# Row means on one core: the loop's loads issued by GpSimd as single packets instead of by SyncE

## The chip, the cores and the metric

The kernel runs on one core of one Trainium2 chip. A core has the engines PE (TensorE, unused here), DVE (VectorE), ACT (ScalarE), POOL (GpSimd) and SP (SyncE), which run their own instruction streams and meet at semaphores, and 16 DMA engines that move data between HBM and the on-chip memory of 128 partitions. The metric is the device time of one execution in microseconds (us). Lower is better.

## The reference

```python
x = np.random.randn(64, 256, 8192).astype(np.float32)

def reference(x):
    return np.mean(x, axis=2)
```

16,384 rows of 8,192 float32 values, 536.87 MB, are read once; 16,384 means are written.

## The kernel before

The 16,384 rows are spread over 128 partitions, 128 rows to each partition. A partition's rows lie in two zones, of 111 and 17 rows, and rows that follow each other in a zone are contiguous in HBM. Two buffers take the rows: `four` holds four rows for each partition (128 KB, 16.78 MB over all), `two` holds two (64 KB, 8.39 MB). There is no second copy of either, so that a load into one runs while the other is being reduced.

SP issues every load, on one hardware queue, in this order:

- three pieces into `two` (a row at the border of the zones and one ahead of it, L109 to L111), then the first `four` load (L112, semaphore `second_sem`);
- the loop of 17 rounds (L114): wait until `two` is free, load two rows into it (L116, `two_sem`), wait until `four` is free, load four rows into it (L118, `four_sem`). Both waits take their count back with a decrement;
- the rest, unrolled (`REST`, L121 to L131): two and four rows in turn, waits with constants; then the last two rows in five chunks that grow shorter (L136), and the two stores.

DVE reduces both rows of `two` with one tensor_reduce (`pair`, L169), then three rows of `four` by adding the halves of a row and accumulating the sum (`quad`, `halves`, L151). In the loop it waits for `two_sem` (L183), reduces, waits for `go_sem` (L185), which ACT raises when `four` has landed, and for `turn_sem` (L186), writes its three sums into `turn`, and copies them to the results (L189). Ahead of the loop DVE reduces the first `two` and then waits for the first `four` load (L179). ACT sums the fourth row of `four` by an activation with an accumulated output (L218), in the loop after a wait on `four_sem` (L224). `two_free` counts finished `pair`s; `four_free` gets one count from DVE and one from ACT for each `four` that is done, and SP waits for both.

GpSimd does little: it sets `turn_sem`, clears one column (L89), and scales the results to means, first the 111 of the large zone (L91, after `four_free` has reached 4 in the rest), then the others (L97).

All of the loop's waits on a load compare with 16, since each load adds 16 to its semaphore, one for each DMA engine, and the waiting engine takes the 16 off again.

Of the kernel before, what the change touches and what calls it, by code (L numbers as in the profile page):

```python
# [11 lines left out]
def bass_global_avg_pool_1d_kernel(  # L12
# [6 lines left out]
    B, C, L = x.shape  # L19
# [8 lines left out]
    FROM = [0, ZONE[0]]  # L28
    EARLY, LATE = ZONE
    ROUNDS = (ZONE[0] - 9) // 6  # L30
    REST = [(112, 2), (106, 4), (114, 2), (116, 4), (120, 2)]
    HALF, LASTP = 122, 124
# [12 lines left out]
    zone = [  # L45
        flat[P * f : P * (f + n), :].rearrange("(p r) l -> p (r l)", p=P)
        for f, n in zip(FROM, ZONE)
    ]
# [5 lines left out]
    with ExitStack() as ctx:  # L54
        sb = lambda n, s: ctx.enter_context(nc.sbuf_tensor(n, s, F32))
        sem = lambda n: ctx.enter_context(nc.semaphore(n))
# [7 lines left out]
        four = sb("four", [P, 4 * L])  # L64
        two = sb("two", [P, 2 * L])

        four_sem = sem("four_sem")
        go_sem = sem("go_sem")
        two_sem = sem("two_sem")
        turn_sem = sem("turn_sem")  # L70
        four_free = sem("four_free")
        two_free = sem("two_free")
        first_sem = sem("first_sem")
        second_sem = sem("second_sem")
        chunk_sems = [sem(f"chunk_sem{c}") for c in range(4)]
        owned_sem = sem("owned_sem")
        last_sem = sem("last_sem")
# [6 lines left out]

        eng = nc.gpsimd
        eng.sem_inc(turn_sem, 2)
        eng.memset(part(NPART - 1), 0.0).then_inc(last_sem, 1)  # L89
        eng.wait_ge(four_free, 4)  # L90
        eng.tensor_scalar(  # L91
            scaled[:], res[:, 0:EARLY], inv, None, op0=mybir.AluOpType.mult
# [8 lines left out]


        eng = nc.sync
        def rows_of(n, k):
            z = 1 if n >= FROM[1] else 0
            return zone[z][:, (n - FROM[z]) * L : (n - FROM[z] + k) * L]

        a, z = rows_of(ZONE[0] - 1, 1), rows_of(ZONE[0], 1)
        eng.dma_start(two[:, L : L + FIRST], z[:, 0:FIRST]).then_inc(first_sem, 16)  # L109
        eng.dma_start(two[:, L + FIRST : 2 * L], z[:, FIRST:L]).then_inc(first_sem, 16)  # L110
        eng.dma_start(two[:, 0:L], a).then_inc(first_sem, 16)  # L111
        eng.dma_start(four[:], rows_of(0, 4)).then_inc(second_sem, 16)  # L112
        src = rows_of(4, 6 * ROUNDS).rearrange("p (i w) -> p i w", i=ROUNDS)
        with eng.Fori(0, ROUNDS) as i:  # L114
            eng.wait_ge(two_free, 1).then_inc(two_free, -1)
            eng.dma_start(two[:], src[:, bass.ds(i, 1), 0 : 2 * L]).then_inc(two_sem, 16)  # L116
            eng.wait_ge(four_free, 2).then_inc(four_free, -2)
            eng.dma_start(four[:], src[:, bass.ds(i, 1), 2 * L : 6 * L]).then_inc(  # L118
                four_sem, 16
            )  # L120
        for k, (n, size) in enumerate(REST):  # L121
            if size == 2:
                eng.wait_ge(two_free, k // 2 + 1)
                eng.dma_start(two[:], rows_of(n, 2)).then_inc(two_sem, 16)
            else:
                eng.wait_ge(four_free, 2 * (k // 2 + 1))
                eng.dma_start(four[:], rows_of(n, 4)).then_inc(four_sem, 16)
        eng.wait_ge(four_free, 6)
        eng.dma_start(four[:, 0 : 2 * L], rows_of(HALF, 2)).then_inc(four_sem, 16)
        eng.wait_ge(two_free, 5)  # L130
        eng.dma_start(two[:], rows_of(LASTP, 2)).then_inc(two_sem, 16)  # L131
        last = rows_of(OWN - 2, 2)
        for c in range(5):
            a, z = cuts[c], cuts[c + 1]
# [12 lines left out]
        eng = nc.vector  # L147
# [20 lines left out]
        def pair(to, ap=two[:]):  # L168
            eng.tensor_reduce(to, rows_in(ap), X, ADD).then_inc(two_free, 1)  # L169

        def quad(to, done=four_free):
            for j, ap in enumerate(to):
                halves(
                    four[:, j * L : (j + 1) * L], ap, done if j == len(to) - 1 else None
                )
# [4 lines left out]
        quad([at(j, 1) for j in range(3)])  # L180
        with eng.Fori(0, ROUNDS) as i:
            now = sums[:, bass.ds(i, 1), :]
            eng.wait_ge(two_sem, 16).then_inc(two_sem, -16)  # L183
            pair(now[:, :, 0:2])
            eng.wait_ge(go_sem, 1).then_inc(go_sem, -1)  # L185
            eng.wait_ge(turn_sem, 2).then_inc(turn_sem, -2)  # L186
            quad([turn[:, j : j + 1] for j in range(3)], turn_sem)
            eng.wait_ge(turn_sem, 1).then_inc(four_free, 1)
            eng.tensor_copy(  # L189
                now[:, :, 2:5], turn[:].rearrange("p (i w) -> p i w", i=1)  # L190
            ).then_inc(turn_sem, 1)
        for k, (n, size) in enumerate(REST):
            eng.wait_ge(two_sem if size == 2 else four_sem, 16 * (k // 2 + 1))
            if size == 4:
                quad([at(n, 1), at(n + 1, 1)])
            elif k < len(REST) - 1:
                pair(at(n, 2))
            else:
                pair(at(n, 1), two[:, 0:L])
        eng.wait_ge(four_sem, 48)  # L200
        eng.tensor_reduce(  # L201
            at(HALF, 2), rows_in(four[:, 0 : 2 * L]), X, ADD
        ).then_inc(owned_sem, 1)
        eng.wait_ge(two_sem, 64)
        eng.tensor_reduce(at(LASTP, 1), two[:, 0:L], X, ADD).then_inc(owned_sem, 1)  # L205
        eng.wait_ge(chunk_sems[0], 16)
        halves(tail[:, 0:L], res[:, OWN - 2 : OWN - 1], owned_sem)
# [7 lines left out]
        eng = nc.scalar  # L215

        def row(ap, to):
            return eng.activation(ap, ap, COPY, accum_out=to)  # L218
# [2 lines left out]
        eng.wait_ge(second_sem, 16)  # L221
        row(fourth, at(3, 1)).then_inc(four_free, 1)
        with eng.Fori(0, ROUNDS) as i:
            eng.wait_ge(four_sem, 16).then_inc(four_sem, -16)  # L224
            eng.sem_inc(go_sem, 1)
            row(fourth, sums[:, bass.ds(i, 1), 5:6]).then_inc(four_free, 1)
        for k, (n, size) in enumerate(REST):
            if size == 4:
                eng.wait_ge(four_sem, 16 * (k // 2 + 1))
                row(four[:, 2 * L : 3 * L], at(n + 2, 1))  # L230
                row(fourth, at(n + 3, 1)).then_inc(four_free, 1)
        eng.wait_ge(two_sem, 48)
        row(second, at(REST[-1][0] + 1, 1)).then_inc(two_free, 1)
        eng.wait_ge(two_sem, 64)
        row(second, at(LASTP + 1, 1)).then_inc(owned_sem, 1)
        for c in range(4):
            eng.wait_ge(chunk_sems[c], 16)
# [31 lines left out]
```

## Time and profile before

| | |
|---|---|
| median of 2 runs | 1242.8 us (1242.71 to 1242.89) |
| the profiled execution's own time | 1243.15 us |
| its span, first to last instruction | 1241.8 us |
| DVE, ACT, POOL busy | 52%, 14%, 0% |
| DMA | one hardware queue, 536.94 MB, 99.8% of 16 engines' span |
| mean rate over the span | 432 GB/s |

How to read the lines of the profile: engines are PE, DVE, ACT, POOL and SP; `SPq` and `DVEq` are the sequencers of SP and DVE, where their waits and DMA issues stand. L118 is line 118 of the kernel. In a timeline a line has its start, its duration, engine, line, operation, output and input, the count of instructions, and in brackets the idle time of the engine before it with what ended that. In the waits a line names who waited for whom, and then the total, the number and the longest of the waits. In the groups a line ends with busy time and mean ns of one, then the idle time before. DMA issues have their size and the median time from issue to landing; a landing is the moment at which the load's semaphore is complete. The page cuts the span into 40 slices of 31 us each.

### The profile page before, as it was taken

How to read it: one execution, taken by the hardware profiler on the slowest of the kernel's cores; microseconds unless marked ns; L12 is line 12 of the kernel's file. 1: busy time of each engine (PE TensorE's matmuls, PEld its weight loads, DVE VectorE, ACT ScalarE, POOL GpSimd, SP SyncE). 2: the span in 40 equal slices, each digit the busy share in tenths (PEclk: the TensorE clock that was granted, in tenths of full speed). 3: DMA queues.
4: the chain of work that ended last, by engine and by line, in shares of the span. 5: the costliest groups of instructions: out<-in, count | busy, mean ns of one | idle time of the engine just before them, and what ended most of it. 6: DMA issues, size and time to landing. Idle time of an engine off the chain costs nothing. (4 is left out here: it accounts for less than half of the span.)

```text
span 1241.8 us, 713 instructions
## 1 busy us (share of the span) xinstructions
DVE 643.0 (52%) x166; ACT 176.5 (14%) x57; POOL 2.3 (0%) x7
## 2 busy tenths in 40 slices
DVE  2373836454544637383736454554638383625257
ACT  0021020202020202012020202020202102040423
POOL 0000000000000000000000000000000000000000
DMA  9999999999999999999999999999999999999998
GB/s 405 439 439 439 439 431 414 439 439 439 439 439 422 422 439 439 439 439 439 422 422 439 439 439 439 439 422 422 439 439 439 439 439 424 420 439 439 439 439 374
DMA packets 10048, 536.94 MB, mean 432 GB/s; under 512 B 1088, under 2 KB 1216, under 8 KB 1472
## 3 DMA queue, kind: packets, MB, share of 16 engines
q1 hardware_dynamic: 10048, 536.94, 99.8%
HBM read 536.87 MB, written 0.07 MB: 432 GB/s over the span
## 5 line engine op out<-in xcount | busy, mean ns | idle before, releaser
L151 DVE CUSTOM_DVE_ANT_0 four<-four 128x4096 f32<-128x4096 f32 (+3 forms) x62 | 260.5, 4248 | 434.7 <-DVEq L186 366.7
L169 DVE TENSOR_REDUCE res<-two 128x16384 f32 (+2 forms) x21 | 353.1, 16814 | 145.4 <-DVEq L183 96.3
L218 ACT ACTIVATE four<-four 128x8192 f32<-128x8192 f32 x22 | 154.6, 7029 | 1017.9 <-ACTq L224 864.3
L201 DVE TENSOR_REDUCE res<-four 128x2 f32<-128x16384 f32 x1 | 17.2, 17220 | 10.6 <-DMA four<-in_x_dram 10.6
L218 ACT ACTIVATE two<-two 128x8192 f32<-128x8192 f32 x2 | 14.1, 7030 | 36.7 <-DMA two<-in_x_dram 36.7
L205 DVE TENSOR_REDUCE res<-two 128x1 f32<-128x8192 f32 x1 | 8.7, 8686 | 2.1 <-DMA two<-in_x_dram 2.1
L240 ACT ACTIVATE four<-four 128x2048 f32<-128x2048 f32 (+3 forms) x4 | 4.1, 1030 | 7.7 <-DMA four<-in_x_dram 7.5
L189 DVE COPY res<-turn 128x3 f32 x17 | 2.9, 170 | 4.2 <-DVE turn L151 4.2
L151 DVE DVE_READ_ACCUMULATOR2_ANT turn<- 128x1 f32 x51 | 4.2, 83 | 0.0
L218 ACT ACTIVATION_READ_ACCUMULATOR four<-four (+1 forms) x22 | 4.1, 187 | 0.0
L91 POOL TENSOR_SCALAR scaled<-res 128x111 f32<-128x111 f32 x1 | 0.5, 503 | 1117.6 <-ACT four L218 1117.6
L97 POOL TENSOR_SCALAR ends<-res 128x16 f32<-128x16 f32 x1 | 1.5, 1499 | 117.9 <-DVE res L151 117.9
L218 ACT ACT_TABLE_LOAD x1 | 1.3, 1283 | 0.7 <-PEq L254 0.7
L240 ACT ACTIVATION_READ_ACCUMULATOR four<-four 128x1 f32 x4 | 0.7, 186 | 0.0
L151 DVE DVE_READ_ACCUMULATOR2_ANT res<- 128x1 f32 x8 | 0.7, 82 | 0.0
L151 DVE CUSTOM_DVE_ANT_0 fin<-fin 128x228 f32<-128x228 f32 x1 | 0.4, 397 | 0.2 <-ACT four L240 0.2
L218 ACT ACTIVATION_READ_ACCUMULATOR two<-two 128x1 f32 x2 | 0.4, 186 | 0.0
L151 DVE DVE_READ_ACCUMULATOR2_ANT fin<- 128x1 f32 x3 | 0.2, 82 | 0.0
L254 POOL MEMSET const-bfloat16-1.0<- 128x1 bf16 x1 | 0.1, 101 | 0.0
L254 POOL MEMSET const-uint8-127<- 128x1 uint8 x1 | 0.1, 101 | 0.0
L254 POOL MEMSET const-float32-0.0<- 128x1 f32 x1 | 0.1, 99 | 0.2 <-issue 0.2
L89 POOL MEMSET fin<- 128x1 f32 x1 | 0.1, 98 | 0.4 <-POOLq L254 0.4
(2 smaller groups left out, 0.2 us busy)
## 6 DMA issues: line engine op xcount, KB each, us to landing
four<-in_x_dram SPq DMA_DIRECT2D x1, 5120.0 KB, 41.6
two<-in_x_dram SPq DMA_DIRECT2D x1, 4096.0 KB, 20.9
two<-in_x_dram SPq DMA_DIRECT2D x1, 3072.0 KB, 11.7
four<-in_x_dram SPq DMA_DIRECT2D x1, 1920.0 KB, 45.7
two<-in_x_dram SPq DMA_DIRECT2D x1, 1024.0 KB, 4.9
four<-in_x_dram SPq DMA_DIRECT2D x1, 640.0 KB, 46.8
four<-in_x_dram SPq DMA_DIRECT2D x21, 44.1
two<-in_x_dram SPq DMA_DIRECT2D x21, 40.2
```

The source lines that it names most:

```text
L89: eng.memset(part(NPART - 1), 0.0).then_inc(last_sem, 1)
L91: eng.tensor_scalar(scaled[:], res[:, 0:EARLY], inv, None, op0=mybir.AluOpType.mult).then_inc(pool_sem, 1)
L97: eng.tensor_scalar(ends[:, 0 : LATE - 1], res[:, EARLY : OWN - 1], inv, None, op0=mybir.AluOpType.mult,).then_inc(late_sem, 1)
L151: made = eng.tensor_tensor_reduce(ap[:, 0:n], ap[:, 0:n], ap[:, n : 2 * n], scale=scale, scalar=0.0, op0=ADD, op1=ADD, accum_out=to,)
L169: eng.tensor_reduce(to, rows_in(ap), X, ADD).then_inc(two_free, 1)
L189: eng.tensor_copy(now[:, :, 2:5], turn[:].rearrange("p (i w) -> p i w", i=1)).then_inc(turn_sem, 1)
L201: eng.tensor_reduce(at(HALF, 2), rows_in(four[:, 0 : 2 * L]), X, ADD).then_inc(owned_sem, 1)
L205: eng.tensor_reduce(at(LASTP, 1), two[:, 0:L], X, ADD).then_inc(owned_sem, 1)
L218: return eng.activation(ap, ap, COPY, accum_out=to)
L240: eng.activation(ap, ap, COPY, accum_out=part(c)).then_inc(last_sem, 1)
L254: nc = _bacc.Bacc("TRN2", target_bir_lowering=False, num_devices=1)
```

## The change

GpSimd issues the 34 loads of the loop, on its own queue whose descriptors software writes, with the flag `single_packet`, by which all the descriptors that one DMA engine gets for a load form one packet. (A load gives each of the 16 engines 8 partitions: 8 pieces of 64 KB for `two`, 16 for `four`, and the semaphore's increment.) The order of waits in GpSimd's loop is that of SP's loop before. SP keeps the loads ahead of the loop, then waits for a semaphore `handoff`, which GpSimd raises behind its last issue, and goes on with the rest.

A load of the software queue does not share its semaphore with one of the hardware queue, and its semaphore is not decremented: so the loads of the rest get `two_late` and `four_late`, and in the loop DVE and ACT wait for 16 times the number of the round, a value that comes from a register. ACT's increment of `go_sem` moves from an instruction of its own onto its wait.

```diff
         eng = nc.gpsimd
         eng.sem_inc(turn_sem, 2)
         eng.memset(part(NPART - 1), 0.0).then_inc(last_sem, 1)
+        src = rows_of(4, 6 * ROUNDS).rearrange("p (i w) -> p i w", i=ROUNDS)
+        with eng.Fori(0, ROUNDS) as i:
+            eng.wait_ge(two_free, 1).then_inc(two_free, -1)
+            eng.dma_start(
+                two[:], src[:, bass.ds(i, 1), 0 : 2 * L], single_packet=True
+            ).then_inc(two_sem, 16)
+            eng.wait_ge(four_free, 2).then_inc(four_free, -2)
+            eng.dma_start(
+                four[:], src[:, bass.ds(i, 1), 2 * L : 6 * L], single_packet=True
+            ).then_inc(four_sem, 16)
+        eng.sem_inc(handoff, 1)
         eng.wait_ge(four_free, 4)
         eng.tensor_scalar(
             scaled[:], res[:, 0:EARLY], inv, None, op0=mybir.AluOpType.mult
...
         eng = nc.sync
...
         eng.dma_start(four[:], rows_of(0, 4)).then_inc(second_sem, 16)
-        src = rows_of(4, 6 * ROUNDS).rearrange("p (i w) -> p i w", i=ROUNDS)
-        with eng.Fori(0, ROUNDS) as i:
-            eng.wait_ge(two_free, 1).then_inc(two_free, -1)
-            eng.dma_start(two[:], src[:, bass.ds(i, 1), 0 : 2 * L]).then_inc(two_sem, 16)
-            eng.wait_ge(four_free, 2).then_inc(four_free, -2)
-            eng.dma_start(four[:], src[:, bass.ds(i, 1), 2 * L : 6 * L]).then_inc(
-                four_sem, 16
-            )
+        eng.wait_ge(handoff, 1).then_inc(handoff, -1)
         for k, (n, size) in enumerate(REST):
             if size == 2:
                 eng.wait_ge(two_free, k // 2 + 1)
-                eng.dma_start(two[:], rows_of(n, 2)).then_inc(two_sem, 16)
+                eng.dma_start(two[:], rows_of(n, 2)).then_inc(two_late, 16)
             else:
                 eng.wait_ge(four_free, 2 * (k // 2 + 1))
-                eng.dma_start(four[:], rows_of(n, 4)).then_inc(four_sem, 16)
+                eng.dma_start(four[:], rows_of(n, 4)).then_inc(four_late, 16)
...
         with eng.Fori(0, ROUNDS) as i:
             now = sums[:, bass.ds(i, 1), :]
-            eng.wait_ge(two_sem, 16).then_inc(two_sem, -16)
+            eng.wait_ge(two_sem, 16 * i + 16)
             pair(now[:, :, 0:2])
...
         with eng.Fori(0, ROUNDS) as i:
-            eng.wait_ge(four_sem, 16).then_inc(four_sem, -16)
-            eng.sem_inc(go_sem, 1)
+            eng.wait_ge(four_sem, 16 * i + 16).then_inc(go_sem, 1)
             row(fourth, sums[:, bass.ds(i, 1), 5:6]).then_inc(four_free, 1)
```

More of the change, by code (lines that the diff above doesn't have):

```diff
@@ L70, in bass_global_avg_pool_1d_kernel @@
         turn_sem = sem("turn_sem")
+        two_late = sem("two_late")
+        four_late = sem("four_late")
         four_free = sem("four_free")
@@ L74, in bass_global_avg_pool_1d_kernel @@
         second_sem = sem("second_sem")
+        handoff = sem("handoff")
         chunk_sems = [sem(f"chunk_sem{c}") for c in range(4)]
@@ L83, in bass_global_avg_pool_1d_kernel, with rows_of @@
         part = lambda n: fin[:, LAST + n : LAST + n + 1]
+        def rows_of(n, k):
+            z = 1 if n >= FROM[1] else 0
+            return zone[z][:, (n - FROM[z]) * L : (n - FROM[z] + k) * L]
         eng = nc.gpsimd
@@ L103, in bass_global_avg_pool_1d_kernel @@
         eng = nc.sync
-        def rows_of(n, k):
-            z = 1 if n >= FROM[1] else 0
-            return zone[z][:, (n - FROM[z]) * L : (n - FROM[z] + k) * L]
         a, z = rows_of(ZONE[0] - 1, 1), rows_of(ZONE[0], 1)
@@ L123, in bass_global_avg_pool_1d_kernel @@
                 eng.wait_ge(two_free, k // 2 + 1)
-                eng.dma_start(two[:], rows_of(n, 2)).then_inc(two_sem, 16)
+                eng.dma_start(two[:], rows_of(n, 2)).then_inc(two_late, 16)
             else:
                 eng.wait_ge(four_free, 2 * (k // 2 + 1))
-                eng.dma_start(four[:], rows_of(n, 4)).then_inc(four_sem, 16)
+                eng.dma_start(four[:], rows_of(n, 4)).then_inc(four_late, 16)
         eng.wait_ge(four_free, 6)
-        eng.dma_start(four[:, 0 : 2 * L], rows_of(HALF, 2)).then_inc(four_sem, 16)
+        eng.dma_start(four[:, 0 : 2 * L], rows_of(HALF, 2)).then_inc(four_late, 16)
         eng.wait_ge(two_free, 5)
-        eng.dma_start(two[:], rows_of(LASTP, 2)).then_inc(two_sem, 16)
+        eng.dma_start(two[:], rows_of(LASTP, 2)).then_inc(two_late, 16)
         last = rows_of(OWN - 2, 2)
@@ L192, in bass_global_avg_pool_1d_kernel @@
         for k, (n, size) in enumerate(REST):
-            eng.wait_ge(two_sem if size == 2 else four_sem, 16 * (k // 2 + 1))
+            eng.wait_ge(two_late if size == 2 else four_late, 16 * (k // 2 + 1))
             if size == 4:
@@ L199, in bass_global_avg_pool_1d_kernel @@
                 pair(at(n, 1), two[:, 0:L])
-        eng.wait_ge(four_sem, 48)
+        eng.wait_ge(four_late, 48)
         eng.tensor_reduce(
@@ L203, in bass_global_avg_pool_1d_kernel @@
         ).then_inc(owned_sem, 1)
-        eng.wait_ge(two_sem, 64)
+        eng.wait_ge(two_late, 64)
         eng.tensor_reduce(at(LASTP, 1), two[:, 0:L], X, ADD).then_inc(owned_sem, 1)
@@ L228, in bass_global_avg_pool_1d_kernel @@
             if size == 4:
-                eng.wait_ge(four_sem, 16 * (k // 2 + 1))
+                eng.wait_ge(four_late, 16 * (k // 2 + 1))
                 row(four[:, 2 * L : 3 * L], at(n + 2, 1))
                 row(fourth, at(n + 3, 1)).then_inc(four_free, 1)
-        eng.wait_ge(two_sem, 48)
+        eng.wait_ge(two_late, 48)
         row(second, at(REST[-1][0] + 1, 1)).then_inc(two_free, 1)
-        eng.wait_ge(two_sem, 64)
+        eng.wait_ge(two_late, 64)
         row(second, at(LASTP + 1, 1)).then_inc(owned_sem, 1)
```

## The prediction

> **What bounds the kernel now.** I read the page first: the busy shares, the 40 slices, the DMA queue.
>
> ```profile
> span 1241.8 us, 713 instructions
> DVE 643.0 (52%) x166; ACT 176.5 (14%) x57; POOL 2.3 (0%) x7
> DMA  9999999999999999999999999999999999999998
> DMA packets 10048, 536.94 MB, mean 432 GB/s; under 512 B 1088, under 2 KB 1216, under 8 KB 1472
> q1 hardware_dynamic: 10048, 536.94, 99.8%
> ```
>
> No compute engine is busy for much more than half of the span, while the 16 DMA engines are busy from the first slice to the last. There is one queue, and its packets fill 99.8% of the span, so at most 0.2% of 1241.8, 2.5 us, are gaps between packets. The input is 64 x 256 x 8192 x 4 bytes = 536.87 MB, or 8192 pieces of 64 KB; with some small ones that agrees with 10048 packets only if the profile counts every 64 KB piece as a packet of its own.
>
> Then the windows, cut at the rounds of the loop, and the timeline of the first two rounds. The columns of the windows are stretch, busy time of DVE, ACT and POOL, clock, DMA share and GB/s.
>
> ```profile
> 98.16:156.12 57.96, 30.52 (x8) 7.12 (x2) 0.00 (x0) 1.00 1.00 434
> 156.12:1025.20 869.08, 457.72 (x120) 106.85 (x30) 0.00 (x0) 1.00 1.00 434
> ```
>
> ```profile
> 40.05 0.35 SPq L116 DMA_DIRECT2D two<-in_x_dram  x1
> 61.19 7.03 ACT L218 ACTIVATE four<-four 128x8192 f32<-128x8192 f32 x1 [59.19 <-DMA four<-in_x_dram]
> 61.19 4.42 DVE L151 CUSTOM_DVE_ANT_0 four<-four 128x4096 f32<-128x4096 f32 x1 [21.41 <-DMA four<-in_x_dram]
> ...
> 74.55 0.39 SPq L118 DMA_DIRECT2D four<-in_x_dram  x1
> 80.73 17.22 DVE L169 TENSOR_REDUCE res<-two 128x16384 f32 x1 [6.41 <-DVEq L183]
> 98.19 0.33 SPq L116 DMA_DIRECT2D two<-in_x_dram  x1
> 119.38 7.03 ACT L218 ACTIVATE four<-four 128x8192 f32<-128x8192 f32 x1 [51.07 <-ACTq L224]
> ...
> 132.93 0.38 SPq L118 DMA_DIRECT2D four<-in_x_dram  x1
> 138.69 17.22 DVE L169 TENSOR_REDUCE res<-two 128x16384 f32 x1 [5.63 <-DVEq L183]
> 156.15 0.34 SPq L116 DMA_DIRECT2D two<-in_x_dram  x1
> ```
>
> A round moves 6 rows of 32 KB on 128 partitions, 25.17 MB, in 57.96 us: 434.2 GB/s, in the second round as in the fifteen after it. A `four` load (16.78 MB) takes 38.64 us of the queue, a `two` load (8.39 MB) 19.32. The compute engines only wait for landings, and those of one queue come in the order of issue: `four` at 61.19, `two` at 80.73, `four` at 119.38, `two` at 138.69. The queue stays full because each load is issued while the other runs. With `two` this has 21 us to spare (issued at 40.05, the running load lands at 61.19). With `four` it is close: issued at 132.93, when the load ahead lands at 138.69, 5.76 us later. How long a load takes from an empty queue to its landing, beyond its bytes, comes from the first issue of all:
>
> ```profile
> two<-in_x_dram SPq DMA_DIRECT2D x1, 1024.0 KB, 4.9
> four<-in_x_dram SPq DMA_DIRECT2D x21, 44.1
> ```
>
> 1024 KB at 434.2 GB/s are 2.4 us, so 2.5 us lie outside the bytes, with nothing ahead. Queued behind a running load they are hidden, if the issue comes 2.5 us early: the `four` issue has 5.76 - 2.5 = 3.3 us to spare.
>
> **The change part by part.** All of it is reckoned against the profiled execution's own 1243.15 us (span 1241.8), which is 0.35 above the median of 1242.8.
>
> The bytes, the sizes and the destinations stay. SP loses 34 issues of 0.33 to 0.39 us; it only waits between them, so that is worth nothing. GpSimd gets them.
>
> ```profile
> L97 POOL TENSOR_SCALAR ends<-res 128x16 f32<-128x16 f32 x1 | 1.5, 1499 | 117.9 <-DVE res L151 117.9
> DVE res L169 <- DVEq L183: 96.3, 17, 6.4
> DVE four L151 <- DVEq L186: 366.7, 17, 21.6
> ```
>
> ```profile
> L118 SPq FUSED_REGOPS  x17: 42/43/43, 74.4 to 1002.1; - x17
> ```
>
> What a load costs when GpSimd issues it, no row shows; call the time beyond SP's x. From below it is -0.4, an issue that costs nothing. From above I take 3.3, where the loop starts to lose. The nearest row is GpSimd's own slowest instruction, 1.5 us against SP's 0.39, so x = 1.1. In the loop this is covered by the 3.3 us of the `four` issue and 21 us of the `two` issue: nothing. GpSimd's two scalings stand behind the loop, and the first of them ran at 1118 us, long after the loop's last issue (1002.20, below): nothing. The waits of DVE and ACT now compare with a value from a register. SP needs 43 ns for a register step (the median of the three figures in the last row); DVE stands 5.6 us before each `two` load (L183) and longer before each `four` load (L186), so this is hidden too. The two semaphores for the rest only rename waits. One packet for 8 or 16 pieces can save at most the gaps, 2.5 us, if the pace inside the packets stays, and every long stretch has the same 434; I take 0, and keep -2.5 for the range.
>
> Two places remain where one queue hands over to the other. The end first:
>
> ```profile
> 1002.20 0.38 SPq L118 DMA_DIRECT2D four<-in_x_dram  x1
> 1007.94 17.22 DVE L169 TENSOR_REDUCE res<-two 128x16384 f32 x1 [5.62 <-DVEq L183]
> 1025.19 0.34 SPq L124 DMA_DIRECT2D two<-in_x_dram  x1
> 1046.73 4.42 DVE L151 CUSTOM_DVE_ANT_0 four<-four 128x4096 f32<-128x4096 f32 x1 [21.57 <-DVEq L186]
> ...
> 1118.52 0.50 POOL L91 TENSOR_SCALAR scaled<-res 128x111 f32<-128x111 f32 x1 [1117.62 <-ACT four L218]
> ```
>
> SP waits for the handoff, with all the later loads behind that wait; it comes with GpSimd's last issue, where SP's stands at 1002.20, and SP's next load waits until 1025.19 for its buffer: 23 us of cover. At that moment the last `four` load of the loop runs on the software queue with 21.5 us to go. If it is one packet for each DMA engine, the engines finish it, and the new `two` load follows. Nothing lost.
>
> The start is the other way round. At 40 us GpSimd issues its first `two` load. The hardware queue still holds 21 us of SP's first `four` load, in pieces of 64 KB that are packets of their own. If a DMA engine takes turns between two queues, packet by packet, it takes the software queue's packet next, all 8 pieces of it, and the remaining pieces of `four` after that. The total of the bytes is the same, so it is `four` that lands at 80.7, and `two` near 62. But DVE and ACT need `four` first: DVE waits for it ahead of the loop, and only GpSimd's next issue, `four` again, could refill the queue. Step by step:
>
> From the landing of `four` to the next `four` issue it was 74.55 - 61.19 = 13.36 us, so now 80.7 + 13.4 = 94.1. By then both loads are down and the queues are empty. This issue lands 2.5 + 38.64 + x later, at 135.2 + x, where it landed at 119.38: 15.9 + x late. DVE reduces the waiting `two` buffer from 94.1 to 111.4, its next load queues behind the running one, and from there the rounds have the old shape. Nothing later has slack to give this back, since the queue was never idle. With x = 1.1: 17.0 us.
>
> The Trainium skill ("DMA: Bandwidth & Descriptors", Queues, rings and completion order) says that each engine goes round between the queues that hold work and changes only at packet boundaries. By that the sum is the one below; no run here shows two queues yet.
>
> Sum: 1243.15 - 0.35 + 17.0 = 1259.8. With x from -0.4 to 3.3 and a gain of up to 2.5, this case lies between 1256 and 1262.
>
> **The rivals.** *No overtaking.* The engines finish what the hardware queue holds at 40 us before they look at the other. Then only the gaps are in play: 1242.8 - 2.5 to 1242.8 + 1, say 1240 to 1244, not slower than before. It decides by how late `four` lands: the refill comes too late once 61.2 + 13.4 + 2.5 + delay passes 80.7, so from a delay of 3.6 us. For it: the profile's count may be one of pieces, and SP's whole load one packet for each engine, which would be finished first. (The same section of the Trainium skill calls 9 to 17 descriptors a typical packet, and SP's `four` load gives each engine about that many; no row here decides it.) Against it: 16 engines each hold some eight of those pieces when the second queue begins.
>
> *The packet is not kept whole.* If the software queue's load also goes piece by piece, the start costs the same (both loads end near 80.7), and the end pays too: the `two` load issued at 1025.19 mixes with the rest of the last `four` load, which lands near 1065 in place of 1046.7, and the next `four` issue finds the queue empty as above, another 15.9 us, SP's own. 1259.8 + 15.9 = 1275.7.
>
> *GpSimd's issue is slow.* Beyond x = 3.3 each of the 16 later `four` issues leaves a gap of x - 3.3. With x = 5: 16 x 1.7 + 15.9 + 5 = 48, 1291. It passes 2% (24.9 us) from x of about 3.8. Against it: 1.5 us for a whole instruction of GpSimd.
>
> *DVE keeps GpSimd from issuing.* The issue at 94.1 falls together with a reduce of 17.22 us. If GpSimd had to wait for it, the queue would be empty for 17.2 us more: 1277. In the loop the `four` issue falls into DVE's 5.6 us of waiting, and the `two` issue follows the end of a reduce, so nothing more there. The Trainium skill ("SBUF — State Buffer", Who interferes with whom) warns that descriptors written by GpSimd are held up while DVE has their shared port, above all in copies, and says that a tensor reduce does not take it on trn2; by that this rival falls, and no row here tests it.
>
> **How the numbers follow.** Overtaking at the start 0.56 (1260); no overtaking 0.24 (1240 to 1244); a faster pace that no row shows 0.01; packet not whole 0.06 (1276); slow issue 0.08 (over 1268); DVE in the way 0.05 (1277). The first two hold 0.8, and the range takes both with their bounds, 1239 to 1265; the likeliest alone is 1256 to 1262. About 2% is what a measurement of this kernel can tell from no change. Faster by over 2% means under 1218, which 536.87 MB at 434.2 GB/s (1236.5 us) exclude unless the pace rises: 0.01. Slower by over 2% is above 1267.7: 0.06 + 0.08 + 0.05 = 0.19. Within 2%: 0.80.
>
> **What would show it.** In the profile after: ACT's first row reduction starts near 80.7 instead of 61.2, and the first reduce of the loop's `two` follows at 94; the GB/s of the fourth slice (62 to 93 us) fall to about half, with one gap of some 17 us between 79 and 97; all later slices are as before, and the last load of the loop lands in order. A first start of ACT at 61 would show that nothing was overtaken; a dip in every round, a slow issue; a second gap near 1080 us, a packet that isn't whole. The forecast is wrong if the rounds are not 57.96 us long, or if the two queues keep the order of issue.

## The result and the profile after

The changed kernel takes 1273.64 us (two runs, 1273.52 to 1273.77) against 1242.8: 1.0248 of the time before, with a 95% interval of 1.0204 to 1.0292. It is 30.8 us slower. The forecast was 1259.8, and its range ended at 1265.

The page of the changed kernel, in the lines that answer to those of before, and the GB/s of the 40 slices, each 31.8 us long:

```profile
span 1272.6 us, 681 instructions
DMA  9959999999999999999999999999999999699998
GB/s 428 428 231 428 428 455 435 428 428 428 428 459 431 428 428 428 437 451 431 428 428 428 447 443 428 428 428 428 459 431 428 428 428 396 264 428 428 439 445 371
q0 software_dynamic: 7072, 427.82, 77.6%
q1 hardware_dynamic: 2976, 109.12, 19.9%
```

The bytes are the same, in two queues now. There are two holes and no more: the third slice (231 GB/s) and the 34th and 35th (396 and 264). Both queues' packets number 7072 + 2976 = 10048, as before: the profile still counts each 64 KB piece by itself. In the windows of the changed kernel (stretch, busy time of DVE, ACT and POOL, clock, DMA share, GB/s), cut at the two holes and at the rounds between them, nothing else has changed:

```profile
78.00:97.00 19.00, 19.00 (x7) 7.08 (x2) 0.73 (x1) 1.00 0.29 110
97.00:133.67 36.67, 11.21 (x1) 0.00 (x1) 0.57 (x1) 1.00 0.99 429
191.69:945.00 753.31, 396.70 (x104) 92.60 (x27) 16.44 (x26) 1.00 1.00 434
1080.20:1096.00 15.80, 15.40 (x8) 7.12 (x2) 0.00 (x0) 1.00 0.20 66
```

The thirteen rounds from 191.69 to 945.00 take 57.95 us each at 434 GB/s, as they did. The timeline shows the first hole from inside:

```profile
40.46 0.73 POOL L100 DMA_DIRECT2D two<-in_x_dram  x1 [39.43 <-POOLq L99]
77.95 7.03 ACT L225 ACTIVATE four<-four 128x8192 f32<-128x8192 f32 x1 [75.82 <-DMA four<-in_x_dram]
...
91.00 17.21 DVE L176 TENSOR_REDUCE res<-two 128x16384 f32 x1
91.84 0.73 POOL L104 DMA_DIRECT2D four<-in_x_dram  x1 [50.66 <-POOLq L103]
108.96 0.57 POOL L100 DMA_DIRECT2D two<-in_x_dram  x1 [16.39 <-POOLq L99]
133.67 7.03 ACT L225 ACTIVATE four<-four 128x8192 f32<-128x8192 f32 x1 [48.59 <-DMA four<-in_x_dram]
```

SP's first `four` load, on the way since 2.2 us, lands at 77.95 where it landed at 61.19. DVE and ACT wait for it, `two` stays full, and the next load goes out at 91.84 into empty queues. The loop's first `four` lands at 133.67, where it landed at 119.38: 14.3 us late.

The second hole is the handover to SP:

```profile
1002.99 7.03 ACT L225 ACTIVATE four<-four 128x8192 f32<-128x8192 f32 x1 [50.87 <-DMA four<-in_x_dram]
...
1017.05 0.70 POOL L104 DMA_DIRECT2D four<-in_x_dram  x1 [34.28 <-POOLq L103]
1022.25 17.22 DVE L176 TENSOR_REDUCE res<-two 128x16384 f32 x1 [5.59 <-DMA two<-in_x_dram]
1039.50 0.34 SPq L131 DMA_DIRECT2D two<-in_x_dram  x1
1080.19 7.03 ACT L225 ACTIVATE four<-four 128x8192 f32<-128x8192 f32 x1 [70.08 <-DMA four<-in_x_dram]
...
1093.54 0.38 SPq L134 DMA_DIRECT2D four<-in_x_dram  x1
...
1135.26 7.03 ACT L225 ACTIVATE four<-four 128x8192 f32<-128x8192 f32 x1 [47.95 <-DMA four<-in_x_dram]
```

The same two landings in the timeline of before, the loop's last `four` and the first one of the rest:

```profile
1046.59 7.03 ACT L218 ACTIVATE four<-four 128x8192 f32<-128x8192 f32 x1 [50.82 <-ACTq L224]
...
1104.31 7.03 ACT L218 ACTIVATE four<-four 128x8192 f32<-128x8192 f32 x1 [50.59 <-DMA four<-in_x_dram]
```

In the changed kernel the loop's last `four` load should land 57.95 us after the one before it (1002.99), at 1060.9. It lands 19.3 us later, the time of a whole `two` load. The load that follows it lands at 1135.26 instead of 1104.31: 30.95 late in all. Of these the loop was 14.35 late until then (1002.99 against 988.64), so 16.6 us came from this handover. They are fewer than 19.3 because the load that follows goes out at 1093.54 into empty queues and lands after 41.7 us, where it stood behind a `two` load before and took 44.3. Sum: 14.3 + 16.6 = 30.9.

How the two loads shared the engines at each place is read from the landings and, below, from the packets. The answers for the single instructions give their duration and start, and the time from issue to landing:

```profile
L100 POOL DMA_DIRECT2D two<-in_x_dram x1: 727/727/727, 40.5 to 40.5; - x1
...
DMA to landing us min/median/max: 39.9/39.9/39.9
```

```profile
L131 SPq DMA_DIRECT2D two<-in_x_dram x1: 339/339/339, 1039.5 to 1039.5; - x1
...
DMA to landing us min/median/max: 40.7/40.7/40.7
```

At the start `two` lands at 40.46 + 39.9 = 80.4, one piece of 64 KB (2.4 us) after `four` at 77.95. Had the software queue's load gone as a whole, it would have landed near 62 and `four` last. At the end both land at the same moment, 1080.2. That is what two loads look like that take turns, piece by piece, to the end.

The DMA view of short stretches shows the turns themselves. A line of it has the queue and the packets that start in the stretch, their MB, and their time as a share of 16 engines. The stretches are 45.7 to 48.1, 48.1 to 50.5 and 77.15 to 79.6 us:

```profile
q0 software_dynamic: 16, 1.05, 100.8%
...
q1 hardware_dynamic: 16, 1.05, 100.8%
...
q0 software_dynamic: 16, 1.05, 98.7%
q1 hardware_dynamic: 16, 0.00, 0.4%
```

There are 16 packets of 64 KB from GpSimd's `two`, one for each engine, then 16 from SP's `four`, and so on. From 45.7 to 77.2 us GpSimd's queue starts 112 packets, seven for each engine. Seven of the 16 pieces that make 38.64 us are 16.9 us, and `four` is 16.76 us late. The third stretch shows that the semaphore's increments are packets too, and wait their turn: the last data of `four` starts before 74.7, and its 16 increments (0.00 MB) come only after GpSimd's seventh pieces.

### The profile page after: what moved, and what is told of

Read it like the earlier page. It is cut to its first block, busy times and chain, and to the rows that moved or that the text cites. A ratio compares the mean times of both kernels' runs of the same rounds, so it can differ in the third digit from the quotient of the medians.

```text
span 1272.6 us, 681 instructions
## 1 busy us (share of the span) xinstructions
DVE 642.9 (51%) x166; ACT 176.5 (14%) x57; POOL 24.0 (2%) x41
## 2 busy tenths in 40 slices
DMA packets 10048, 536.94 MB, mean 422 GB/s; under 512 B 1088, under 2 KB 1216, under 8 KB 1472
## 3 DMA queue, kind: packets, MB, share of 16 engines
q0 software_dynamic: 7072, 427.82, 77.6%
q1 hardware_dynamic: 2976, 109.12, 19.9%
## 5 line engine op out<-in xcount | busy, mean ns | idle before, releaser
L104 POOL DMA_DIRECT2D four<-in_x_dram x17 | 11.9, 698 | 602.5 <-POOLq L103 602.5
L100 POOL DMA_DIRECT2D two<-in_x_dram x17 | 9.8, 577 | 392.5 <-POOLq L99 392.5
## 6 DMA issues: line engine op xcount, KB each, us to landing
four<-in_x_dram SPq DMA_DIRECT2D x1, 5120.0 KB, 41.7
two<-in_x_dram POOLq DMA_DIRECT2D x17, 39.9
```

What stands on the lines that cost most here:

```text
L100: eng.dma_start(two[:], src[:, bass.ds(i, 1), 0 : 2 * L], single_packet=True).then_inc(two_sem, 16)
L104: eng.dma_start(four[:], src[:, bass.ds(i, 1), 2 * L : 6 * L], single_packet=True).then_inc(four_sem, 16)
```

## The experiments

The theory after the result (A): any two queues of a core take turns at each DMA engine, one piece each, and the flag does not change that. What it costs is decided by which load is held up: a `four` load, which the next issue waits for, or a `two` load, which has 21 us to spare. The rivals stand in the expectations. The kernel before, run beside these, had medians of 1242.95 to 1243.01.

**The flag alone.**

```diff
-                two[:], src[:, bass.ds(i, 1), 0 : 2 * L], single_packet=True
+                two[:], src[:, bass.ds(i, 1), 0 : 2 * L]
...
-                four[:], src[:, bass.ds(i, 1), 2 * L : 6 * L], single_packet=True
+                four[:], src[:, bass.ds(i, 1), 2 * L : 6 * L]
```

> Only the flag single_packet is taken away from the 34 loads. Theory A (the two queues take turns piece by piece, 64 KB at a time, with the flag or without): 1273.6 us within 0.5, the first four load lands near 78, the last one of the loop near 1080. Theory B (the flag holds a part of a load together, and the loss at the end comes from the hardware queue going first): without the flag the first four load lands at another time than 78, or the loss at the end changes by several us. Theory C (the flag makes the pieces flow faster, and the two handovers hide it): the rounds get longer than 57.95 us.

Measured: 1273.64 us, the changed kernel's time to 0.01. The first `four` load of the kernel without the flag:

```profile
78.23 7.03 ACT L225 ACTIVATE four<-four 128x8192 f32<-128x8192 f32 x1 [76.10 <-DMA four<-in_x_dram]
```

That is 0.3 us from the landing with the flag. The packets alternate in the same way, 16 of GpSimd's from 45.9 to 48.3 us and 16 of SP's from 48.3 to 50.7. The rounds take (1003.44 - 133.78) / 15 = 57.98 us, against 57.95. Nothing that the change gained or lost came from the flag; theories B and C fall.

**The start handed over at the other load.** SP issues the first round's `two`, and GpSimd begins with that round's `four`. DVE's first round is written out, since its `two` has another semaphore.

```diff
-        with eng.Fori(0, ROUNDS) as i:
+        eng.wait_ge(four_free, 2).then_inc(four_free, -2)
+        eng.dma_start(four[:], rows_of(6, 4), single_packet=True).then_inc(four_sem, 16)
+        eng.wait_ge(two_free, 2).then_inc(two_free, -1)
+        with eng.Fori(1, ROUNDS) as i:
...
         eng = nc.sync
...
+        eng.wait_ge(two_free, 1)
+        eng.dma_start(two[:], rows_of(4, 2)).then_inc(round_sem, 16)
         eng.wait_ge(handoff, 1).then_inc(handoff, -1)
...
```

> SP issues the two load of the first round, GpSimd begins with that round's four load, so that the software queue starts behind a two load, which has 21 us to spare, and not behind a four load. Theory A (what costs is that a load that is needed soon shares the engines with one that is not): the first loss, 14.3 us, goes, 1259.3 us within 1; the second, 16.6 us, stays. Rival (the first use of the software queue costs some 14 us wherever it comes): 1273.6 us.

Measured: 1259.85 us, ratio 1.0136 [1.0117, 1.0154]. The first loss is gone, 13.8 of 14.3 us: the loop's first `four` lands at 119.38, as it did in the kernel before. The second loss stays, with the loop's last two `four` landings 77.2 us apart (988.78 and 1065.99).

**The end handed over at the other load.** GpSimd also issues the first `two` load of the rest, so SP begins with a `four` load; the counts of `two_late` shift by one load.

```diff
+        eng.wait_ge(two_free, 1)
+        eng.dma_start(two[:], rows_of(REST[0][0], 2), single_packet=True).then_inc(
+            two_sem, 16
+        )
         eng.sem_inc(handoff, 1)
...
```

> GpSimd issues the first two load of the rest as well, so that SP takes over with a four load, behind a two load that has time to spare. Theory A: the second loss goes, 1273.6 - 16.6 = 1257.0 us within 1, with the first loss kept. Rival (SP's own queue needs time to be taken up again after the software queue): about 1273 us.

Measured: 1257.35 us, ratio 1.0116 [1.0097, 1.0134]. The second loss is gone, 16.3 of 16.6 us: the loop's last two `four` loads land 57.9 us apart (1003.08 and 1061.00). The first loss is there as before, with the loop's first `four` at 133.77.

**Both handed over at the other load.**

> Both handovers are moved as in the two kernels before. Theory A: both losses go, and the loads by GpSimd are worth nothing by themselves: 1242.8 us within 1 (the median of the kernel before). Rival 1 (one packet closes the gaps between pieces): 1240.3 us, 2.5 less. Rival 2 (an issue by GpSimd costs the loop, some tenths of a us in each round): 1246 us or more.

Measured: 1243.14 us (11 runs) against 1242.98, ratio 1.0002 [0.9993, 1.0011]. The 34 loads by GpSimd, with the flag, are worth nothing and cost nothing beyond the interval, some 1 us to either side: rivals 1 and 2, at 2.5 us less and 3 more, both fall. What a packet of several pieces would be worth is not shown by this, since the flag joined none. Two queues still share here. The timeline of this kernel:

```profile
75.08 0.90 POOL L100 DMA_DIRECT2D four<-in_x_dram  x1 [74.06 <-POOLq L99]
83.01 17.22 DVE L188 TENSOR_REDUCE res<-two 128x2 f32<-128x16384 f32 x1 [8.61 <-DMA two<-in_x_dram]
```

The `two` load lands at 83.0 instead of 80.7, held up by 2.3 us, about the time of one piece. What waits is its increments: its last data starts before 79.8 us, from there to 82.2 only GpSimd's 16 packets start, and the increments come behind them. The queue never empties, so nothing is lost.

**Smaller pieces on GpSimd's queue**, 32 KB instead of 64, once with the flag and once without.

```diff
-                two[:], src[:, bass.ds(i, 1), 0 : 2 * L], single_packet=True
+                two[:], src[:, bass.ds(i, 1), 0 : 2 * L], single_packet=True, max_dma_last_dim=32768
...
-                four[:], src[:, bass.ds(i, 1), 2 * L : 6 * L], single_packet=True
+                four[:], src[:, bass.ds(i, 1), 2 * L : 6 * L], single_packet=True, max_dma_last_dim=32768
```

> GpSimd's loads in pieces of 32 KB instead of 64, with the flag. Theory A (a turn is one piece, whatever its size): at the start some 7 pieces of the software queue went ahead of the last piece of four, 16.75 us; at half their size that is 8.4 us, so four lands near 69.6 and the first loss shrinks by 8.4 to about 6; at the end the 8 pieces of SP's two load still go ahead, the second loss stays. 1273.6 - 8.4 = 1265.3 us within 2. Rival (the engines share by bytes, not by pieces): 1273.6 us. Rival (32 smaller pieces cost pace): above that.

> The same pieces of 32 KB without the flag. Theory A: as with it, 1265.3 us within 2. If the flag joins pieces into longer turns, this one is faster than the one with the flag, or that one stays at 1273.6.

Measured: 1267.14 us with the flag, 1267.25 without, both within the 2 us, at its edge. The first `four` load and the loop's first and last but one, with the flag:

```profile
69.66 7.03 ACT L225 ACTIVATE four<-four 128x8192 f32<-128x8192 f32 x1 [67.53 <-DMA four<-in_x_dram]
...
125.47 7.03 ACT L225 ACTIVATE four<-four 128x8192 f32<-128x8192 f32 x1 [48.69 <-DMA four<-in_x_dram]
...
996.46 7.03 ACT L225 ACTIVATE four<-four 128x8192 f32<-128x8192 f32 x1 [50.98 <-DMA four<-in_x_dram]
```

The landing at 69.66 (69.73 without the flag) is the 69.6 of theory A: half the bytes in each turn, half the delay. If the engines shared by bytes, it would have stayed at 78. The missing 1.8 us are in the pace, and so far the last rival was right: (996.46 - 125.47) / 15 = 58.07 us for a round, 0.11 more than the (1002.99 - 133.67) / 15 = 57.95 of the changed kernel, over 16 rounds.

**Small pieces on SP's side of the second handover.** Only the first `two` load of the rest changes.

```diff
-                eng.dma_start(two[:], rows_of(n, 2)).then_inc(two_late, 16)
+                eng.dma_start(
+                    two[:], rows_of(n, 2), max_dma_last_dim=8192 if k == 0 else 65536
+                ).then_inc(two_late, 16)
```

> Only SP's first two load of the rest goes in pieces of 8 KB; all else as in the changed kernel. Theory A: each turn takes 8 KB of it against 64 KB of the last four load of the loop, whose 8 remaining pieces are late by 8 x 8 KB, 2.4 us, less than the 3.3 us that there are to spare: the second loss goes, 1257 us within 1.5. Rival (sharing by bytes, or SP's queue before GpSimd's): 1273.6 us.

Measured: 1257.70 us, ratio 1.0118 [1.0089, 1.0148]. The loop's last two `four` loads in this kernel:

```profile
1003.17 7.03 ACT L227 ACTIVATE four<-four 128x8192 f32<-128x8192 f32 x1 [50.85 <-DMA four<-in_x_dram]
1063.55 7.03 ACT L227 ACTIVATE four<-four 128x8192 f32<-128x8192 f32 x1 [53.26 <-DMA four<-in_x_dram]
```

They are 60.38 us apart, 2.4 more than a round, where they were 77.2 apart. The same bytes come at the same place in the same order; only the size of a turn is smaller, and the loss is gone.

**Two hardware queues.** The kernel before, with one load moved: ACT issues the first `two` load of the rest, ahead of its last round, which is taken out of the loop.

```diff
-        with eng.Fori(0, ROUNDS) as i:
+        with eng.Fori(0, ROUNDS - 1) as i:
...
+        eng.wait_ge(handoff, 1).then_inc(handoff, -1)
+        eng.wait_ge(two_free, 1)
+        eng.dma_start(two[:], rows_of(REST[0][0], 2)).then_inc(act_sem, 16)
...
```

> The kernel before, with one load alone moved: the first two load of the rest is issued by ACT, on a second hardware queue, at the same moment as SP would. No software queue is in it. Theory A (any second queue shares piece by piece): four lands some 19 us late, the loss at the end comes back, 1243.0 + 16.6 = 1259.6 us within 1. Rival (only the software queue and a hardware queue mix in this way): 1243 us.

Measured: 1259.51 us, ratio 1.0133 [1.0103, 1.0162]. The one load moved and the `four` load beside it:

```profile
1025.16 0.37 ACTq L239 DMA_DIRECT2D two<-in_x_dram  x1
1065.81 7.03 ACT L228 ACTIVATE four<-four 128x8192 f32<-128x8192 f32 x1 [70.06 <-ACTq L240]
```

`four` lands at 1065.81 where SP's single queue landed it at 1046.59. The packets alternate here too: 16 of ACT's queue from 1028.5 to 1031.0 us, 16 of SP's from there to 1033.4. Moving one load of 50 to a second queue costs 16.5 us, with no software queue in the program.

**The flag on small pieces.** One doubt was left: the flag might hold pieces together only up to some length. So GpSimd loads `two` as two halves in pieces of 8 KB, 32 for each engine and load.

```diff
-            eng.dma_start(
-                two[:], src[:, bass.ds(i, 1), 0 : 2 * L], single_packet=True
-            ).then_inc(two_sem, 16)
+            for h in range(2):
+                eng.dma_start(
+                    two[:, h * L : (h + 1) * L],
+                    src[:, bass.ds(i, 1), h * L : (h + 1) * L],
+                    single_packet=True, max_dma_last_dim=8192,
+                ).then_inc(two_sem, 16)
...
-            eng.wait_ge(two_sem, 16 * i + 16)
+            eng.wait_ge(two_sem, 32 * i + 32)
```

> GpSimd loads two as two halves, each in pieces of 8 KB (32 pieces for each DMA engine and load), with the flag; four stays in pieces of 64 KB. Theory A (a turn is one piece, the flag changes nothing in that): at the start some 7 turns of 8 KB go ahead of the last piece of four, 2.1 us, less than there is to spare: the first loss goes, 1273.6 - 14.3 = 1259.3 us within 1.5, as without the flag. Rival (the flag does hold small pieces together, and fails only on packets as long as those of the changed kernel): 32 pieces, 256 KB, to a turn, four lands near 80 as before, 1273 us.

> The same without the flag. Theory A: 1259.3 us within 1.5, and the same landing of the first four load within 0.5 us as with the flag. Rival: 1259 us here, and 1273 with the flag.

Measured, one run each: 1263.98 us with the flag, 1264.24 without. The landings with the flag, the first `four`, the loop's first, and the last but one:

```profile
63.41 7.03 ACT L228 ACTIVATE four<-four 128x8192 f32<-128x8192 f32 x1 [61.28 <-DMA four<-in_x_dram]
...
119.92 7.03 ACT L228 ACTIVATE four<-four 128x8192 f32<-128x8192 f32 x1 [49.38 <-DMA four<-in_x_dram]
...
993.26 7.03 ACT L228 ACTIVATE four<-four 128x8192 f32<-128x8192 f32 x1 [51.11 <-DMA four<-in_x_dram]
```

and the first without it:

```profile
63.42 7.03 ACT L228 ACTIVATE four<-four 128x8192 f32<-128x8192 f32 x1 [61.29 <-DMA four<-in_x_dram]
```

and the packets with it, from 46.0 to 48.75 us:

```profile
q1 hardware_dynamic: 16, 1.05, 87.9%
q0 software_dynamic: 16, 0.13, 11.2%
```

Each engine takes one piece of 64 KB and one of 8 KB in this stretch. The first `four` is 2.2 us late, the 2.1 of turns of 8 KB, and the same without the flag: it doesn't hold 32 small pieces together either. The first loss is gone (119.92 against 119.38 before). The total missed the expectation of 1259.3 by 4.7 us, and the reason stands in the rounds: (993.26 - 119.92) / 15 = 58.22 us, 0.27 more than 57.95, 4.3 us over 16 rounds; the loop's first `four` was 0.5 us late.

## Why the prediction was wrong

*The bound* held: one set of engines at 434.2 GB/s, rounds of 57.95 us before and after, and a time that moved only where the queues ran empty.

*The step that failed* is the one at the end: "If it is one packet for each DMA engine, the engines finish it, and the new `two` load follows. Nothing lost." It took the flag at its word, as the account of the change does, which says that by it all of a load's descriptors for one engine form one packet. The load was not kept whole, in this run or in any other with the flag; SP's pieces went between GpSimd's, the last `four` of the loop lost 19.3 us and the kernel 16.6. The prediction's own sign of this came: a second gap near 1080 us. The rival "The packet is not kept whole" had this place, its mechanism and 1275.7 us, 2.1 from the result, but a chance of 0.06 and a time outside the range. Nothing in the trace of before spoke for the flag, as nothing spoke against it; with one queue only, no row could. A step whose only support is the meaning of a flag deserves more than 0.06 on its failure.

*The start* had the right wait and, by the same false step, the wrong turn. The forecast had all of `two` go first in one turn, so that `four` would land at 80.7; with turns of one piece it lands one piece ahead of the end, at 77.95. That is the difference between 17.0 forecast and 14.3 measured. That the price came so near is luck of the sizes: seven pieces went ahead where eight were forecast, and both loads end near 80 either way, which the rival had noted.

*Two slips* changed nothing: the stretch from 62 to 93 us is the third slice of the page, not the fourth, and with the prediction's own terms a slow issue passes 2% from x of about 3.6, not 3.8.

*GpSimd's issue* was sized well: x = 1.1 was taken. The issue starts 13.89 us after the landing instead of 13.36, and the row of the 17 `four` issues in the changed kernel, with the shortest, median and longest time to landing, gives the rest:

```profile
L104 POOL DMA_DIRECT2D four<-in_x_dram x17: 696/696/726, 91.8 to 1017.1; - x17
...
DMA to landing us min/median/max: 41.6/43.7/62.9
```

The shortest, 41.6, is the one into empty queues, against 2.5 + 38.64 = 41.1: 0.5 + 0.5 = 1.0 us. So the rival of a slow issue falls: the loop had 3.3 us to spare and did not change.

*DVE in the way* falls too. That issue at 91.84 came 0.84 us into a tensor reduce of 17.21 us (91.00, above) and landed 41.6 us later; waiting for the reduce's end would have added 16 us. The Trainium skill ("SBUF — State Buffer", Who interferes with whom) says that a tensor reduce does not contend with GpSimd on trn2; this run agrees for one issue. What it says of copies was not tested.

*The gain of one packet* was put at 0, with up to 2.5 for the range. Measured: 0.16 us slower with both handovers moved, within the interval. The runs do not show whether a joined packet would gain, since none was joined.

*Packets and turns.* The Trainium skill ("DMA: Bandwidth & Descriptors", Queues, rings and completion order) says that an engine changes queues only at packet boundaries, and calls 9 to 17 descriptors a typical packet. The runs agree with the first if every piece is a packet of its own, as the profile counts them: on the hardware queues at 8 and 64 KB, on the software queue at 8, 32 and 64 KB, with the flag or without. They show no packet of several pieces anywhere.

*Open:* why the flag does nothing. It may not reach the descriptors, or the engines may change queues inside a packet; both would give these turns and landings, and no run here tells them apart.

## What to carry to other kernels

A second queue is no second lane: each load in flight gives up one turn for every turn of the newcomer, so the older load is late by as much of the newer one as fits beside it. Hand over from one queue to another where the load in flight is the one that has time to spare, or give the newcomer small pieces; at the second handover each of the two took away some 16 us, with the same bytes. Small pieces in every round have a price, told below. And this kernel, whose DMA engines are busy for 99.8% of its span, had at most 2.5 us of gaps to win from the way its loads are issued, while the two handovers lost 14.3 and 16.6.

## What the runs showed of the hardware

A turn is one descriptor's piece, at each size that was tried, and the increment of a load's semaphore takes a turn as well. With pieces of 64, 32 and 8 KB on the software queue, the first `four` load landed at 77.95, 69.66 and 63.41 us, against 61.19 with one queue. So the size of the pieces sets how two queues share: a load in small pieces holds up one in large pieces less.

A piece has a price of its own, with the flag or without. A round in pieces of 64 KB has 24 for each engine and takes 57.95 us. With 24 more (32 KB) it takes 0.11 us more, with 56 more and one more load (8 KB for `two`) 0.27: 4.6 to 4.8 ns for each piece. By that, the 24 pieces of the kernel before cost some 0.11 us in a round, 1.9 us over 17 rounds. This is an estimate from these rows of what joining them could have brought at most; no run joined any.

The software queue moved its rounds at the same 434 GB/s as the hardware queue, in the thirteen that the windows above show.
